# A recurrent layer's front: where the mixed inputs lie, how the second factors run, and how the 32-token blocks are inverted

## The chip, the core and the metric

The kernel runs on one core of a Trainium2 chip. The metric is the device time of one execution in microseconds (us), the median of several runs. Five engines work side by side, each through its own queue in order: TensorE (PE, its weight loads as PEld), VectorE (DVE), ScalarE (ACT), GpSimd (POOL) and SyncE (SP), which issues the loads of the weights.

## The reference, cut

Two blocks follow each other; the second one and most of the first are not touched by the change. What it touches is the time mix of the first block's first layer:

```python
xx = jnp.pad(h, ((0, 0), (1, 0), (0, 0)))[:, :-1] - h
xm = h[None] + xx[None] * mix[:, None, None, :]
xr, xw, xk, xv, xa, xg = xm[0], xm[1], xm[2], xm[3], xm[4], xm[5]
r = xr @ w_r; k = xk @ w_k; v = xv @ w_v
w_log = -jax.nn.softplus(-(w0 + jnp.tanh(xw @ w1) @ w2)) - 0.5
a = jax.nn.sigmoid(a0 + (xa @ a1) @ a2)
kk = (k * k_k).reshape(B, T, H, N)
kk = kk / jnp.maximum(jnp.sqrt(jnp.sum(kk * kk, axis=-1, keepdims=True)), 1e-12)
k = k * (1.0 + (a - 1.0) * k_a)
decay = jnp.exp(-jnp.exp(w_log))
y = wkv7_scan(r, decay, k, v, -kk, kk * a)   # a step for each token, 16 heads of 64
```

There are 272 tokens (16 meta tokens and 256), a width of 1024, 16 heads.

## The kernel before, in words

All activations lie transposed: 128 features on the partitions, 8 tiles `k` or `m` of the width, 272 tokens as columns. A large matrix product is made of *units*. A unit loads 128x1024 weights (`wf`, a ring of 5), ScalarE rounds them to a high part (`wh`, a ring of 4, L173), VectorE takes the difference as a low part (`wl`, a ring of 3, L182), and TensorE runs 24 matmuls, three for each of 8 tiles (L261 to L263). Mixed inputs are split into a high and a low part in the same way: the rounding is ScalarE's, the difference VectorE's (L488). The high part of a unit is made four units ahead, so it waits until an earlier unit has given its buffer back.

The scan over tokens is computed in chunks of 64 tokens. In each chunk the inverse of a unit triangular 64x64 matrix is wanted for every head. The kernel takes it apart into two diagonal blocks of 32 tokens and the square below them. `aab` (L737, L740, eight of them, m = 0 to 7) makes the blocks from the removal keys, `meta` the 16-token block of the meta tokens; `inverses` inverts all 32-token blocks of all heads and chunks at once on VectorE, row by row (`rows`, L862 and L865, and L879 for the last rows); and `doubles` joins two inverted blocks to 64 tokens with two products (`da`, L1116, and `db`, L1124). Behind the joining the chunks follow on TensorE, and all of it waits for it.

The *front* is what lies between the norm and the joining. Its steps stand in a list `ORDER` written out by hand, in which the chunk steps, the units of keys (`k0` to `k7`), values (`v0` to `v7`) and `r` (`r0` to `r7`) and the small steps are strung together. The queues are then ordered from that list by a scheduler, which may move instructions past others where nothing depends.

The steps that matter here:

- `low_rank`, then `lwa`, `lg1`, `lg2`: first factors of decay, rate and gate, and the hyperbolic tangents behind them (L592 to L599).
- `first_mix`: the key's mixed input. A tile is normalised (L529), the difference to the token before is written to `xx` (L531), the mixed tile is `xx * mix + hn` (L533), and it is split (L534, L488). The pair lies in a store with the tag `AR`, the same store in which the decays and unit keys are put later, so the decays' exponentials (`decay_b`, L662 and L663) come behind the last key (`dropk`).
- `mv` and `mr`: mixed inputs of values and of `r`, a tile each; the values from `xx` (L504), `r` from two scaled copies of `hn` (L501, L502).
- `l2w`, `l2a`: second factors of decay and rate (L636), two units that each load the same weights `rk_l2` and use one half of their rows.
- `evk`, `evkb`: a key's square and copy (L616, L239), its heads' squared sums (L623) and their maximum with 1e-24 (L624).
- `decay_a`: sums of the decays along the tokens (L651).
- `units`, `keys`, `keysb`, `removal`, `over`, each for a half (4 tiles) of the width: unit keys (L680, L681, L683), keys times rate (L690, L698), removal keys (L711, L713, L716) and the products with the inverse decays (L705, L707), which `aab` reads.
- `evr`, `evrb`: an `r` unit's read-out and bonus (L777, L778, L786); `solve0` to `solve8`: the steps of `inverses`.

PSUM has 8 buffers, the temporary tiles `t` 3, `s` 4.

## Time and profile before

| what | us |
|---|---|
| median of 3 runs (1541.54 to 1544.8) | 1543.73 |
| the profiled execution | 1541.39 |
| its span, first to last instruction | 1539.4 |
| PE busy, share of the span | 1477.2, 96% |
| DVE busy | 1008.7, 66% |
| ACT busy | 747.2, 49% |
| POOL busy | 263.5, 17% |
| mean granted clock | 0.984 |

All times of instructions below come from the one profiled execution; 2.0 us of its time lie around the span. A busy PE counts instructions in flight, and matmuls overlap, so a mean duration of a matmul is longer than the distance to the next one. An instruction's duration holds a start-up that overlaps with its neighbour, so the distance from one start to the next is what a queue pays. Float32 matmuls leave two records each, the ones with rounded parts (fp32r) one.

### The profile page before, as it was taken

How to read it: one execution, taken by the hardware profiler on the slowest of the kernel's cores; microseconds unless marked ns; L12 is line 12 of the kernel's file. 1: busy time of each engine (PE TensorE's matmuls, PEld its weight loads, DVE VectorE, ACT ScalarE, POOL GpSimd, SP SyncE). 2: the span in 40 equal slices, each digit the busy share in tenths (PEclk: the TensorE clock that was granted, in tenths of full speed). 3: DMA queues.
4: the chain of work that ended last, by engine and by line, in shares of the span. 5: the costliest groups of instructions: out<-in, count | busy, mean ns of one | idle time of the engine just before them, and what ended most of it. 6: DMA issues, size and time to landing. Idle time of an engine off the chain costs nothing.

```text
span 1539.4 us, 31043 instructions
## 1 busy us (share of the span) xinstructions
PE 1477.2 (96%) x12652; PEld 1404.3 (91%) x12652; DVE 1008.7 (66%) x1893; ACT 747.2 (49%) x1295; POOL 263.5 (17%) x298
## 2 busy tenths in 40 slices
PE   7999999678999999999999998999999999999999
PEld 7999998677789999999999986789999988899999
DVE  6657567996666555556555489576665589887643
ACT  6545436633255444444444344555454236666532
POOL 2111000111012111011110234141110344310000
PEclk9999999888999999999999999999999999999999
DMA  7655643222105555555555531065556543265553
GB/s 221 219 175 177 194 130 122 72 83 70 43 2 183 174 179 167 171 196 177 169 172 168 179 124 55 28 198 194 185 182 181 185 142 95 90 221 191 188 194 98
DMA packets 71874, 230.62 MB, mean 150 GB/s; under 512 B 8851, under 2 KB 13492, under 8 KB 71604
## 3 DMA queue, kind: packets, MB, share of 16 engines
q1 hardware_dynamic: 69504, 225.35, 45.4%
q10 hardware_dynamic: 2228, 3.29, 0.9%
q8 instruction: 99, 1.62, 0.4%
q14 instruction: 43, 0.35, 0.1%
HBM read 226.52 MB, written 2.10 MB: 149 GB/s over the span
## 4 chain that ended last, share of the span: by engine, by line
PE 84%; DVE 9%; ACT 3%; DMA 1%; issue 1%; POOL 1%; SPq 0%; DVEq 0%; POOLq 0%; ACTq 0%
PE mm L261 23%; PE mm L263 23%; PE mm L262 23%; PE mm L1890 1%; DVE wl L182 1%; PE mm L1164 1%; PE mm L1163 1%; PE mm L1165 1%; DMA wf<-ffn_in 1%; PE mm L1867 1%; PE mm L988 1%; PE mm L1892 1%; PE mm L1834 1%; PE mm L801 1%; ACT L L1846 1%
## 5 line engine op out<-in xcount | busy, mean ns | idle before, releaser
L173 ACT ACTIVATE wh<-wf 128x1024 fp32r<-128x1024 f32 (+2 forms) x410 | 417.7, 1020 | 549.3 <-issue 264.7
L182 DVE TENSOR_TENSOR wl<-wf,wh 128x1024 fp32r<-128x1024 f32 (+2 forms) x402 | 479.5, 1194 | 142.2 <-PE mm L263 104.0
L261 PE MATMUL mm<-xh,wh 128*128 128x272 f32 (+1 forms) x1824 | 525.7, 288 | 8.3 <-ACT wh L173 8.3
L263 PE MATMUL mm<-xh,wl 128*128 128x272 f32 (+1 forms) x1824 | 523.6, 288 | 2.7 <-DVE wl L182 2.6
L262 PE MATMUL mm<-xl,wh 128*128 128x272 f32 (+1 forms) x1824 | 523.1, 287 | 0.0
L261 PEld LDWEIGHTS mm<-xh,wh 128*128 128x128 f32 x1824 | 345.2, 189 | 11.1 <-ACT wh L173 9.2
L263 PEld LDWEIGHTS mm<-xh,wl 128*128 128x128 f32 x1824 | 344.7, 189 | 4.4 <-DVE wl L182 3.9
L262 PEld LDWEIGHTS mm<-xl,wh 128*128 128x128 f32 x1824 | 344.4, 189 | 0.4
L261 PE MATMUL mm<-hh,wh 128*128 128x272 f32 (+1 forms) x704 | 201.7, 287 | 0.0
L263 PE MATMUL mm<-hh,wl 128*128 128x272 f32 (+1 forms) x704 | 201.6, 287 | 0.0
L262 PE MATMUL mm<-hl,wh 128*128 128x272 f32 (+1 forms) x704 | 201.5, 287 | 0.0
L352 POOL TENSOR_TENSOR s<-s,rstd 128x272 f32<-128x272 f32 (+1 forms) x88 | 75.4, 859 | 443.6 <-ACT s L351 443.6
L261 PEld LDWEIGHTS mm<-hh,wh 128*128 128x128 f32 x704 | 132.6, 188 | 0.0
L263 PEld LDWEIGHTS mm<-hh,wl 128*128 128x128 f32 x704 | 132.5, 188 | 0.0
L262 PEld LDWEIGHTS mm<-hl,wh 128*128 128x128 f32 x704 | 132.4, 188 | 0.0
L360 DVE TENSOR_TENSOR u<-mm,s 128x272 f32<-128x272 f32 (+1 forms) x88 | 38.5, 437 | 118.5 <-PE mm L263 103.2
L182 POOL TENSOR_TENSOR wl<-wf,wh 128x1024 fp32r<-128x1024 f32 (+3 forms) x44 | 85.3, 1943 | 114.7 <-PE mm L263 38.6
L298 POOL TENSOR_TENSOR acc<-acc,sq 128x272 f32<-128x272 f32 (+1 forms) x48 | 41.8, 871 | 253.6 <-ACT sq L296 245.3
L350 DVE TENSOR_TENSOR t<-mm,rstd 128x272 f32<-128x272 f32 (+1 forms) x88 | 38.2, 436 | 66.9 <-PE mm L263 66.8
L261 PE MATMUL mm<-hid,wh 128*128 128x256 f32 x256 | 72.0, 281 | 0.0
L262 PE MATMUL mm<-hid,wh 128*128 128x256 f32 x256 | 72.0, 281 | 0.0
L263 PE MATMUL mm<-hid,wl 128*128 128x256 f32 x256 | 72.0, 281 | 0.0
(492 smaller groups left out, 2313.8 us busy)
## 6 DMA issues: line engine op xcount, KB each, us to landing
wf<-ffn_in SPq DMA_DIRECT2D x176, 512.0 KB, 3.6
wf<-ffn_out SPq DMA_DIRECT2D x64, 512.0 KB, 3.6
wf<-b_ff SPq DMA_DIRECT2D x64, 512.0 KB, 4.4
wf<-ffn_out SPq DMA_DIRECT2D x32, 384.0 KB, 3.2
wf<-rk_k SPq DMA_DIRECT2D x8, 512.0 KB, 3.5
wf<-rk_v SPq DMA_DIRECT2D x8, 512.0 KB, 3.3
wf<-rk_r SPq DMA_DIRECT2D x8, 512.0 KB, 3.4
wf<-rk_o SPq DMA_DIRECT2D x8, 512.0 KB, 3.3
```

Source lines behind the costliest of these rows:

```text
L173: self.A.activation(u.wh, u.wf[:u.p, :u.n], AF.Copy)
L182: (self.V if u.lo == "V" else self.G).tensor_tensor(u.wl, u.wf[:u.p, :u.n], u.wh.bitcast(F32), op=ALU.subtract)
L261: self.mm(out, wh, xh, start=start, stop=False)
L262: self.mm(out, wh, xl, start=False, stop=False)
L263: self.mm(out, wl, xh, start=False, stop=stop)
L298: self.G.tensor_tensor(self.acc[:, :n], self.acc[:, :n], self.sq[:, :n], op=ALU.add)
L350: V.tensor_tensor(t[:, :n], st.pop(("g", m))[:, :n], r, op=ALU.mult)
L352: G.tensor_tensor(s[:, :n], s[:, :n], r, op=ALU.mult)
L360: V.tensor_tensor(u[:, :n], st.pop(("u", m))[:, :n], st.pop(("s", m))[:, :n], op=ALU.mult)
L801: mm(p[:, :T], wf[:w, s], R["lo"][1 - z][:w], start=z == 0, stop=z == 1)
L988: mm(ps[h][:, j * w:(j + 1) * w], flat(src(c, m)[OWN[h]]), R["AR"][OWN[h], m, j0:j0 + n, tok(c)], start=True, stop=True)
L1163: self.mm(out, xh, wh, start=start, stop=False)
```

## The change

Four edits and a new order.

1. *Key's mixed input.* Its high part gets a slot of its own (`xkh`) and its low part the lower half of the store for the key products (now two halves, `kb0` and `kb1`). The store `AR` is free from the start, so `decay_b` stands behind the fourth key.
2. *No token differences.* Keys, values and `r` are all mixed as `mix * hn_before + (1 - mix) * hn`: a scaled copy on ScalarE and one instruction on VectorE. The tables `1 - mix` are written by GpSimd (`others`) over columns of `vec` that are no longer read.
3. *Second factors in one unit.* `l2` loads the weights once and issues a product for decay and one for rate for each tile.
4. *The maximum with 1e-24* becomes a Relu of the sum less 1e-24 on ScalarE, and 1e-24 is added again in the logarithm.
5. *Inverses in 16-token blocks.* `rows` runs 15 rows, each one instruction pair over both 16-token diagonal blocks. Then the lower square is filled: transposes (`turned`), 128 products of 32x16 (first of them the lower square times the first inverse), a copy and a transpose (`joined`), 192 products, and three instructions that add (`added`).

In the key products `aover` (removal keys) and `over` (keys) are now separate steps, and the meta columns are made for each half.

```diff
-ORDER = ("lwa k0 lg1 k1 evk0 l2w evk1 evkb0 k2 lg2 tri mv mv k3 evk2 evkb1 decay_a mv mv l2a k4 evk3 evkb2 mv k5 evk4 "
+ORDER = ("k0 lwa k1 evk0 k2 lg1 evk1 evkb0 l2 evk2 evkb1 k3 decay_a lg2 tri evk3 evkb2 decay_b k4 mv evk4 evkb3 units0 "
...
+        def mixed(i, k):
+            p, x = self.tmp("s"), self.tmp("t")
+            A.activation(p, R["hn"][:, k, :T], AF.Copy, scale=self.v("mix", 8 * i + k))
+            V.scalar_tensor_tensor(x, R["hn"][:, k, 1:], self.v("mix", 8 * MIX[i] + k), p, op0=ALU.mult, op1=ALU.add)
+            return x
...
-            x2 = R["pool"].tile([128, 2, KT, T], F32R, tag="AR", name="xk")
-            hi, lo = R["x", 2] = x2[:, 0], x2[:, 1]
+            hi = slot("xkh", F32R, (128, KT, T))
+            lo = R["half"](0, "xkl", F32R).rearrange("p (k t) -> p k t", k=KT)
...
-                eng(E("xx%d" % k)).tensor_tensor(xx[:, k], hn[:, k, :T], hn[:, k, 1:], op=ALU.subtract)
...
-                V.tensor_scalar(R["rn"][:, m], ss[:, :T], 1e-24, None, op0=ALU.max)
+                A.activation(R["rn"][:, m], ss[:, :T], AF.Relu, bias=self.eps[:, 4:5])
...
+                    ps = [self.psum() for _ in range(2)]
+                    for p, r in zip(ps, OWN):
+                        mm(p[:, :T], wf[r, m * 128:m * 128 + 128], R["lo"][0][r], start=True, stop=True)
+                    ev_w(m, ps[0][:, :T])
+                    ev_a(m, ps[1][:, :T])
...
             for s in range(s0, s1):
-                if s < B - 5:
...
+                m, w = n - 1 - s, s + 1
+                u = self.tmp("u")[:, :2 * m * w].rearrange("p (b i j) -> p b i j", b=2, j=w)
+                below = both(t, w, 0, (B, m), (1, w))
+                V.tensor_tensor(u, both(a, s, w, (1, m), (0, w)), both(t, s, 0, (0, m), (1, w)), op=ALU.mult)
+                V.tensor_tensor(below, below, u, op=ALU.add)
...
+        def turned():
+            tf, Dg, Dt = R["tf"], R["Dg"], R["af"]
+            V.transpose(Dg[:, :n], tf[:, :, :n].rearrange("p s t -> p t s"))
+            V.transpose(Dt, tf)
+            p = R["p16"] = self.psum()
+            for c in range(32):
+                for r in quads:
+                    mm(p[r, c * n:c * n + n], Dg[r, :, c], Dg[r, :n, c], start=True, stop=True)
+        def joined():
...
+            V.transpose(Dg[:, n:], tf[:, :, n:].rearrange("p s t -> p t s"))
+            self.A.activation(tf[:, :, :n], byblk(R.pop("p16")), AF.Copy)
+            G.memset(tf[:, :, n:], 0.0)
+            p, o = R["p16"] = self.psum(), self.psum()
+            for c in range(32):
+                for r in quads:
+                    mm(p[r, c * n:c * n + n], tf[r, c], Dt[r, n:, c], start=True, stop=True)
+                for r in quads[::2]:
+                    mm(o[r, c * n:c * n + n], Dt[r, :, c], tf[r, c, :n], start=True, stop=True)
...
-        cuts = (0, 5, 10, 15, 20, 25, 31)
+        cuts = (0, 5, 10, 15)
```

Three places of the queues show what moves. The first is ScalarE, behind the tangents of decay and rate. Before, the exponentials (L662, L663) stand behind the last keys, after them and a load of the function table; `wh` is a high part, `s` and `kf` a key's square and copy, `kbx` the store of squared sums:

```order
L173 ACTIVATE wh<-wf 128x1024
L616 ACTIVATE s<-mm,vec 128x272
L239 ACTIVATE kf<-mm 128x272
L301 ACT_TABLE_LOAD
L680 ACTIVATE kbx<-kbx 128x1088
L173 ACTIVATE wh<-wf 128x1024
L662 ACTIVATE AR<-pinv 128x8x272
```

In the changed kernel (its own line numbers) the same stretch of ScalarE starts behind the tangents of both factors; L639 are the Relus, L534 the scaled copies, L515 the roundings of the values' mixed input, L674 and L675 the exponentials:

```order
L534 ACTIVATE s<-hn,vec 128x272
L639 ACTIVATE kb<-mm,eps 128x272
L303 ACT_TABLE_LOAD
L674 ACTIVATE AR<-pinv 128x8x272
L175 ACTIVATE wh<-wf 128x1024
L630 ACTIVATE s<-mm,vec 128x272
L241 ACTIVATE kf<-mm 128x272
L534 ACTIVATE s<-hn,vec 128x272
L515 ACTIVATE xmh<-t 128x272
L534 ACTIVATE s<-hn,vec 128x272
L639 ACTIVATE kb<-mm,eps 128x272
L675 ACTIVATE pinv<-pinv 128x8x272
```

The exponentials have moved ahead of the fifth key's square, and the values' mixing stands between the keys' squares.

The second place is VectorE at the end of the solve. Before, the last rows (L865, L879) are mixed with read-outs of `r` units (L777, L778) and a low part, and two transposes (L885, L886) end it:

```order
L862 TENSOR_TENSOR u<-af,tf 128x81
L865 TENSOR_TENSOR tf<-tf,u 128x2x27
L777 SCALAR_TENSOR_TENSOR s<-mm,vec,kf 128x272
L778 TENSOR_TENSOR AR<-mm,AR 128x272
L865 TENSOR_TENSOR tf<-tf,u 128x3x27
L182 TENSOR_TENSOR wl<-wf,wh 128x1024
L879 SCALAR_TENSOR_TENSOR tf<-tf,af 128x28
L1048 TENSOR_TENSOR room<-mm,pc 128x256
L879 SCALAR_TENSOR_TENSOR tf<-tf,af 128x28 x3
```

In the changed kernel the last rows (L900, L901) stand beside the low parts of the last tiles of `r`'s mixed input (L504), the transposes are L909 and L910, and the first read-outs of `r` (L792, L793) come behind them:

```order
L901 TENSOR_TENSOR tf<-tf,u 128x2x3x13
L504 TENSOR_TENSOR xl<-t,xh 128x272 x2
L900 TENSOR_TENSOR u<-af,tf 128x56
L504 TENSOR_TENSOR xl<-t,xh 128x272
L901 TENSOR_TENSOR tf<-tf,u 128x2x2x14
L900 TENSOR_TENSOR u<-af,tf 128x30
L901 TENSOR_TENSOR tf<-tf,u 128x2x15
L909 STREAM_TRANSPOSE tf<-tf 128x512
L910 STREAM_TRANSPOSE af<-tf 128x1024
L792 SCALAR_TENSOR_TENSOR s<-mm,vec,kf 128x272
```

The third is TensorE at the joining. Before, the fifth `r` unit ends, a chunk product (L1042) follows, and L1116 is the next:

```order
L262 MATMUL mm<-xl,wh 128x272
L263 MATMUL mm<-xh,wl 128x272
L1042 MATMUL mm<-UV,KBt 64x64 x8
L1116 MATMUL mm<-tf,Tt 32x32 x16
L1042 MATMUL mm<-UV,KBt 64x64 x8
L1116 MATMUL mm<-tf,Tt 32x32 x8
L786 MATMUL mm<-s,mats 128x272
```

In the changed kernel the first new batch (L914) stands behind the second `r` unit, with a bonus product (L801) and the third unit behind it:

```order
L264 MATMUL mm<-xl,wh 128x272
L265 MATMUL mm<-xh,wl 128x272
L914 MATMUL mm<-tf 32x16 x128
L801 MATMUL mm<-s,mats 128x272
L263 MATMUL mm<-xh,wh 128x272
L264 MATMUL mm<-xl,wh 128x272
```

The second batch (L924 and L926 in turn, 32 times four and two) stands behind that third unit and the meta products (L1055); then come the fourth unit, two chunk products (L1067, L1084), two bonus products, the fifth unit, L1095 (which was L1042) and L1168 (which was L1116). So the whole solve lies between the second and the fifth `r` unit on TensorE, and from L1168 on both queues hold the same instructions.

## Rows read from the trace of the kernel before

**Rows 1.** Table by stage: busy us (and records) per engine, then PEclk.

```profile
core 0: us, PE busy (x) PEld busy (x) DVE busy (x) ACT busy (x) POOL busy (x), PEclk, DMA share, GB/s
220.00:230.00 10.00, 10.00 (x82) 10.00 (x82) 9.76 (x26) 1.73 (x4) 0.00 (x0) 1.00 0.00 1
229.60:291.56 61.96, 50.42 (x339) 45.89 (x337) 49.33 (x96) 46.40 (x85) 4.01 (x8) 0.93 0.35 117
...
302.45:357.35 54.90, 39.27 (x612) 36.53 (x613) 53.89 (x208) 15.67 (x28) 8.96 (x14) 0.85 0.28 87
357.35:371.31 13.96, 12.38 (x188) 10.30 (x188) 5.04 (x14) 7.37 (x13) 4.16 (x4) 0.61 0.01 2
```

**Rows 2.** What TensorE waited for, 215 to 372 us: total, times, longest.

```profile
PE mm L737 <- DVE AR L716: 12.5, 2, 9.1
PE mm L786 <- DVE s L777: 8.1, 1, 8.1
PE mm L1116 <- DVE tf L885: 5.9, 1, 5.9
```

**Rows 3.** VectorE's groups, 216 to 366 us: busy us, mean ns, idle before.

```profile
L182 DVE TENSOR_TENSOR wl<-wf,wh 128x1024 fp32r<-128x1024 f32 x21 | 25.5, 1219 | 8.7 <-issue 5.2 <-PE mm L263 2.0 <-ACT wh L173 1.4
...
L865 DVE TENSOR_TENSOR tf<-tf,u 128x110 f32<-128x110 f32 (+32 forms) x54 | 11.8, 253 | 0.1
L862 DVE TENSOR_TENSOR u<-af,tf 128x110 f32<-128x110 f32 (+32 forms) x54 | 11.5, 256 | 0.0
...
L624 DVE TENSOR_SCALAR kbx<-mm 128x272 f32<-128x272 f32 x8 | 3.5, 432 | 0.3 <-PE mm L623 0.3
...
L531 DVE TENSOR_TENSOR kbx<-hn 128x272 f32<-128x272 f32 x8 | 3.4, 440 | 0.0
...
L885 DVE STREAM_TRANSPOSE tf<-tf 128x1024 f32<-128x1024 f32 x1 | 1.9, 1905 | 0.0
...
L879 DVE SCALAR_TENSOR_TENSOR tf<-tf,af 128x28 f32<-128x28 f32 (+3 forms) x10 | 1.8, 231 | 0.0
```

**Rows 4.** VectorE's timeline before the fifth block: start, us, instruction.

```profile
295.23 1.30 DVE L698 TENSOR_TENSOR kf<-kf,kbx 128x1088 f32<-128x1088 f32 x1
296.43 1.30 DVE L711 SCALAR_TENSOR_TENSOR tha<-tha,AR 128x1088 f32<-128x1088 f32 x1
297.63 0.51 DVE L502 SCALAR_TENSOR_TENSOR t<-hn,hv,s 128x272 f32<-128x272 f32 x1
298.04 0.80 DVE L488 TENSOR_TENSOR xl<-t,xh 128x272 fp32r<-128x272 f32 x2
...
300.29 1.44 DVE L705 TENSOR_TENSOR kbx<-tha,pinv 128x256 f32<-128x256 f32 x4
...
301.96 1.43 DVE L716 TENSOR_TENSOR AR<-AR 128x252 f32<-128x252 f32 x4
```

**Rows 5.** ScalarE's timeline behind the first keys: start, us, instruction.

```profile
239.13 1.06 ACT L173 ACTIVATE wh<-wf 128x1024 fp32r<-128x1024 f32 x1 [3.62 <-PE mm L262]
240.09 0.47 ACT L616 ACTIVATE s<-mm,vec 128x272 f32<-128x272 f32 x1
...
240.74 2.00 ACT L645 ACTIVATE pinv<-mm,hv 128x272 f32<-128x272 f32 x5
```

**Rows 6.** ScalarE's groups, 216 to 366 us, columns as in rows 3.

```profile
L690 ACT ACTIVATE kbx<-tha,hv 128x272 f32<-128x272 f32 x8 | 4.3, 600 | 3.8 <-DVE AR L683 3.8
...
L501 ACT ACTIVATE s<-hn,vec 128x272 f32<-128x272 f32 x8 | 3.9, 511 | 0.0
...
L663 ACT ACTIVATE pinv<-pinv 128x2176 f32<-128x2176 f32 x1 | 2.0, 2017 | 0.0
```

**Rows 7.** Narrow float32 products in TensorE's timeline: start, us, instruction, records.

```profile
324.04 0.69 PE L1002 MATMUL mm<-AR,kbx 64*16 64x16 f32 x64
...
343.09 1.07 PE L1031 MATMUL mm<-room,Tm 16*16 16x64 f32 x32
...
370.76 0.62 PE L1124 MATMUL mm<-af,H 32*32 32x32 f32 x16
```

**Rows 8.** The weight loads of L1116, group of 216 to 366 us.

```profile
L1116 PEld LDWEIGHTS mm<-tf,Tt 32*32 32x32 f32 x80 | 2.6, 144 | 6.1 <-issue 6.0
```

**Rows 9.** Table by stage for 14 matmuls of an `r` unit at 1.2 GHz.

```profile
364.89:368.29 3.40, 3.40 (x14) 3.15 (x14) 0.00 (x0) 0.54 (x2) 0.00 (x0) 0.50 0.02 5
```

More of the change, by code (lines that the diff above doesn't have):

```diff
@@ L138, in __init__ @@
         self.later = [(mats, io["mats"]), (self.tri, io["tri"])]
-        self.eps = self.const.tile([128, 2], F32, name="eps")
+        self.eps = self.const.tile([128, 5], F32, name="eps")
         nc.vector.memset(self.eps[:, 0:1], EPS)
         nc.vector.memset(self.eps[:, 1:2], 64e-5)
+        nc.vector.memset(self.eps[:, 3:4], 1e-24)
+        nc.vector.memset(self.eps[:, 4:5], -1e-24)
     def unit(self, *a, **k):
@@ L628, in k_unit, with l2_unit @@
             self.unit(io["rk_k"][m], D, proj(2, m, "k"), lo=E("lok%d" % m), hi=E("hik%d" % m))
-        def l2_unit(j, evac, gen, after=()):
-            r = OWN[j]
+        def l2_unit():
             def fn(wf):
                 for m in range(KT):
-                    p = self.psum()
-                    mm(p[:, :T], wf[r, m * 128:m * 128 + 128], R["lo"][0][r], start=True, stop=True)
-                    evac(m, p[:, :T])
-                    if gen:
-                        next(gen)
-            self.unit(io["rk_l2"], D, fn, after, lo=None)
+                    ps = [self.psum() for _ in range(2)]
[3 more added lines that the diff above has]
+                    ev_a(m, ps[1][:, :T])
+            self.unit(io["rk_l2"], D, fn, lo=None)
         def ev_w(m, p):
@@ L658, in decay_b @@
         def decay_b():
-            AR = R["AR"] = R["pool"].tile([128, NP, 2, T], F32, tag="AR", name="AR")
-            pinv = R["pinv"][:, :, :T]
+            pinv, AR = R["pinv"][:, :, :T], R["AR"]
             with tc.issue_after(R["logs"].ins):
@@ L716, in removal_keys, with removal_over @@
                 V.tensor_tensor(a[:, :, 1:], a[:, :, 1:], p[:, :, :CH - 1], op=ALU.mult)
+        def removal_over(q):
+            over(V, 0, R["tha"], slice(4 * q, 4 * q + 4))
         def keys_over(q):
@@ L835, in rwkv @@
         for q in range(2):
-            for n, fn in (("units", units), ("keys", keys), ("keysb", keys2), ("removal", removal_keys), ("over", keys_over)):
+            for n, fn in (("units", units), ("keys", keys), ("keysb", keys2), ("removal", removal_keys), ("aover", removal_over), ("over", keys_over)):
                 steps[n + str(q)] = lambda fn=fn, q=q: fn(q)
@@ new lines, in rows @@
+                V.tensor_tensor(below, below, u, op=ALU.add)
+        quads = [slice(32 * q, 32 * q + 32) for q in range(4)]
+        byblk = lambda p: p.rearrange("p (c j) -> p c j", j=n)
+        def turned():
[6 more added lines that the diff above has]
+                    mm(p[r, c * n:c * n + n], Dg[r, :, c], Dg[r, :n, c], start=True, stop=True)
@@ new lines, in added @@
+        def added():
+            Dg, Dt = R["Dg"], R["af"]
+            p, o = R.pop("p16")
+            x = Dt[:, n:].rearrange("p t c -> p c t")
+            V.tensor_tensor(x, byblk(p), x, op=ALU.add)
+            for r in quads[::2]:
+                x = Dg[r, :n].rearrange("p t c -> p c t")
+                V.scalar_tensor_tensor(x, byblk(o)[r], self.eps[r, 2:3], x, op0=ALU.mult, op1=ALU.add)
+        def end():
+            R["D1"], R["Dt"] = R["Dg"], R["af"]
+            Tt = R["Tt"]
+            Dt = R["Dt"].rearrange("p t (m c) -> p m c t", c=NC)
@@ L912, in meta @@
                 G.tensor_copy(R["Tm"][:, :, 8 * i:8 * i + 8], x[i][:, :, :KT].rearrange("p t m -> p m t"))
-        cuts = (0, 5, 10, 15, 20, 25, 31)
-        return [start, meta] + [lambda a=a, b=b: rows(a, b) for a, b in zip(cuts[:-1], cuts[1:])] + [end]
+        cuts = (0, 5, 10, 15)
+        return [start, meta] + [lambda a=a, b=b: rows(a, b) for a, b in zip(cuts[:-1], cuts[1:])] + [turned, joined, added, end]
     def chunks(self, R):
@@ L1082, in early @@
         def early():
-            z = R["pool"].tile([128, 2, KT, T], F32R, tag="kbx", name="z")
-            R["z"] = z[:, 0], z[:, 1]
+            z = R["z"] = [R["half"](i, "z", F32R).rearrange("p (k t) -> p k t", k=KT) for i in range(2)]
             e = tok(NC - 1).start
             for q in range(2):
-                self.split(z[:, 0, qs[q], :e], z[:, 1, qs[q], :e], R["bb"][q][:, :, :e], (V, G)[q])
+                self.split(z[0][:, qs[q], :e], z[1][:, qs[q], :e], R["bb"][q][:, :, :e], (V, G)[q])
         steps = {"early": early}
```

92 lines of the change are left out of this document (43 added, 49 removed), and 10 rows, old and new, of the table ORDER.

## The prediction

> **What bounds the kernel now.** I read the table by stage first [rows 1], then what TensorE waited for [rows 2], then the groups of VectorE [rows 3]. TensorE is the bound of nearly the whole program; the exception is the front of the time mix, from 229.6 us (first matmul of a key) to 357.35 us (first product that joins 32-token blocks, L1116). In its first part TensorE is busy 50.42 of 61.96 us, in its last 39.27 of 54.90 us, while VectorE there is busy 53.89 of 54.90 [rows 1]. The waits say the same: 12.5 us in L737 for the removal keys, 8.1 us in L786 and 5.9 us in L1116 for VectorE [rows 2]. After 357.35 the order of both kernels is the same matmul for matmul, so the gain is how much earlier L1116 (L1168 in the new code) starts, plus what the same work takes behind it: 13.96 us up to the first L988 at 371.31, at a granted clock of 0.61 [rows 1], so much of it at 1.2 GHz after the wait of 5.9 us.
>
> **The change part by part.** VectorE loses the differences (L531, 3.4 us) and the maxima (L624, 3.5 us) [rows 3]. The rows of the inverse took 11.8 + 11.5 + 1.8 = 25.1 us [rows 3]: 108 instructions with 96 elements on average (5166 over 54 a side), 0.22 us each, and ten short ones. Now there are 30 with 91 on average (1360 over 15 a side): 30 x 0.21 = 6.3 us. The transposes stay even (one of 1024 in L885's 1.9 us becomes two of 512). ScalarE takes over 16 scalings (8 for the key, 8 for the value) and 8 squared sums.
> One load of 0.5 MB less on SP's queue and the factor tables on GpSimd, written ahead of the front, I cost at nothing: the longest waits there name no transfer [rows 2].
>
> *First, to the first-half removal keys.* The key's mixing ends some 2 us earlier, and three keys then run without a break: 72 matmuls at 0.122 (82 in 10.00 us, [rows 1]) from 229.6, so to 238.4. From 236.9, when the first key is through and the fifth key's high part gets its buffer, ScalarE is the longest queue. What it has up to the keys of the first half (L702): 8 high parts at 0.95 (next start 240.09 behind 239.13), 8 squares with copies at 0.65, 16 tanh at 0.375, 11 scalings at 0.41, 8 roundings at 0.32, two exponentials at 1.9, two passes over 1088 at 1.0, four keys at 0.5 [rows 5, 6], 7 relus at 0.36 taken as such a tanh, a table load 1.3 and a 0.3: 7.6 + 5.2 + 6.0 + 4.5 + 2.6 + 3.8 + 2.0 + 2.0 + 2.5 + 1.6 = 37.8 us, and 1.7 us in which the eighth key's high part waits for TensorE: 276.4 us. Queued behind ScalarE are the values' mixed inputs, so TensorE, done with the keys at 264.4, runs the first three values only as they come, to 276.6.
>
> *Second, to the fifth block product.* From 276.4 VectorE is the longest: 4 low parts at 1.13 [rows 3], three passes over 1088 at 1.2, three copies, 7 mixings, 4 unit keys, and of the key products (L705) four groups of four at 0.33 apiece with their meta pieces, less the last three, and two groups of L716 at 1.45 [rows 4]: 4.5 + 3.6 + 1.1 + 2.5 + 1.7 + 5.0 + 2.9 = 21.3 us. Block 0 may start at about 282 (before 291.6), block 4 at 297.8; before it started at 302.45. Of 9 us at the first only 4.6 are left at the second, since the other half's keys come after. TensorE waits some 5 us ahead of block 0 and 7 ahead of block 4.
>
> *Third, to the first new product.* TensorE from 297.8: block 4, the meta block and its wait 2.1, three blocks 2.9, a value at 1.2 GHz behind the wait 4.4 (14 matmuls took 3.4 at that clock, [rows 9]; at the full one 82 took 10.00, so 24 take 2.9, [rows 1]), three values 8.8, two r units 5.9, two chunk products 3.8: 27.9 us, so 325.7. VectorE meanwhile: blocks and masks to 307, a transpose 2.0, the rows 6.3, the rest of the meta block 1.8, three low parts 3.4, three mixings 2.3, small pieces 1.4, a half transpose 1.0: 325.2 us. They are level; the wait of 8.1 us goes, and nothing as long takes its place.
>
> *Fourth, TensorE alone, to the joining.* New are 128 products (L914) and 192 (L924, L926), 32 rows by 16 columns in float32, of two records each. No row is like them. The nearest from below is L1002, 16 columns: 64 records in 0.69 us, 0.022 us a product. From above L1124, 32 rows and 32 columns, one operand read across as here: 16 records in 0.62, 0.07 to 0.077 a product [rows 7]. Half of L1124's columns gives 0.035, which I take, as the operand and the height are L1124's: 4.5 and 6.7 us (bounds 7 and 24 us for both). Around them one r unit 2.9, two more 5.9, a bonus product 0.5 and two 1.0, meta products 0.7, chunk products 1.9, 1.1 and 0.7: 4.5 + 6.7 + 14.7 = 25.9, so L1168 starts at 351.6, 5.7 us earlier. Copies and memset between the two batches (some 4 us on ScalarE, VectorE and GpSimd) lie beside the r unit, the added pieces beside the next two; without that cover they would cost about those 4 us each time.
>
> *Fifth, behind the joining.* VectorE is done 8 us before L1168, so no wait of 5.9, no drop of the clock, and ScalarE has its four copies behind it. The same matmuls then take 9.8 us for 13.96: 4.1 us less.
>
> Sum: 5.7 + 4.1 = 9.8 us. Each of the eight values' tiles now goes ScalarE, VectorE, ScalarE, VectorE; for hand-offs that my sums leave out I take off 0.2 us a tile, a choice, 1.6 us. That is 8.2 us off the profiled execution's 1541.4: **1533.2**. This execution was the quickest shown; the runs' median is 2.3 higher. Forecast on the middle of both: **1534.5 us**.
>
> A rule of the Trainium skill speaks against the small blocks. L1002's 64 records at 2.4 GHz took 0.011 us apiece with 16 columns, though L1031's took 0.033 with 64 [rows 7]: there the price goes with the columns. The Trainium skill, "TensorEngine Tiling (Array Packing)", section "Instruction Overhead", says that each matmul has about 60 cycles of overhead, so that one column takes as long as 60. By that rule, as an estimate from its figure, 640 records would cost 25 ns each, 16 us and not 11.2. The trace disagrees for L1002, and would agree for L1124 against L1031, where 32 and 64 columns cost the same.
>
> **The rivals.**
> (a) *The products cost by the piece, not by the column.* In [rows 7] L1124 takes as much for 32 columns as L1031 for 64. With a price between, 0.05 a product, the 320 cost 16 us, 4.8 more: about 1539, no change that can be told. (The rule of the Trainium skill's page "TensorEngine Tiling (Array Packing)" gives this case.) Against it: L1002.
> (b) *The products pack like L1002.* Four row groups follow one another, at 0.022: 4.2 us less than the forecast: 1530. For it: the loop over quarters is innermost; against: operands read across.
> (c) *ScalarE holds the front.* Nine microseconds of work went to an engine that was busy 46.40 of 61.96 us [rows 1]. If the key mixing or the hand-offs make its chain 4 to 5 us longer, block 4 starts at 302 as before, and what is left is the shorter solve less the products: 1539. For it: every low part, relu and mixing on VectorE then waits for one queue.
> (d) *Slower: the loads of the strided weights stay in the open.* L914 and L926 load 32 columns that lie 32 elements apart; a load of L1116 lasts 0.144 [rows 8], hidden there. If for these 192 it is not hidden, they cost 0.144 apiece and the other 128 0.035: 32 us, 21 more than the forecast: 1555. Slower from about 0.08 a product on. Against it: in the rows of narrow products the loads are hidden everywhere.
> (e) *The change does not do what it says:* VectorE's four-dimensional patterns run at half the pace, the solve saves 12 and not 19 us, L914 waits for VectorE: 5 us, 1540.
>
> **How the numbers follow.** Forecast 0.52, (b) 0.14, (a) 0.11, (c) 0.11, (d) 0.08, (e) 0.04. A measurement of this kernel tells 0.2%, about 3.1 us, from no change. The forecast with its own range, 1530 to 1539, lies on the faster side but for its edge; with (b) and the lower parts of (a) and (c) that gives faster 0.72, the same 0.18 (most of (a), (c), (e)), slower 0.10 ((d), and a bad end of (c)). The range reaches down to (b) with 3 us for the sums and up to (a), (c) and (e) with 3 above: 1527 to 1543; (d) is left out.
>
> **What would show it.** Block 0 some 9 us earlier and block 4 some 4 to 5 us earlier; ScalarE without gaps from 237 to 276; no wait of 8 us on a VectorE instruction of the r units; the two batches at 4 to 5 and 6 to 7 us; the first L1168 at about 352 us of the span and no clock of 0.61 behind it. Wrong first of all if the batches take over 16 us together, or if TensorE's waits ahead of blocks 0 and 4 come to over 20 us.

## The result, and the profile after

The changed kernel is slower. Its runs took 1551.0 to 1559.2 us, median 1556.4; the kernel before took 1541.5 to 1544.9 on the same chip, median 1544.3; the ratio is 1.0071, with a 95% interval of 1.0046 to 1.0097. The forecast was 1534.5, in a range of 1527 to 1543. The execution in the trace is the quickest of the changed kernel, 1551.0 us with a span of 1549.2, against 1541.4 and 1539.4 before.

The table by stage of the changed kernel, in the columns of [rows 1] (busy us and records per engine, then PEclk, DMA share and GB/s), cut at block 0, block 4, the first batch of narrow products (L914), its end, the second batch (L924, L926), its end, the first product that joins 32-token blocks (L1168, before L1116) and the first L1041 (before L988):

```profile
core 0: us, PE busy (x) PEld busy (x) DVE busy (x) ACT busy (x) POOL busy (x), PEclk, DMA share, GB/s
230.47:284.94 54.47, 46.41 (x315) 41.76 (x313) 38.04 (x69) 48.12 (x93) 2.83 (x8) 0.97 0.30 95
284.94:300.87 15.93, 7.10 (x217) 6.80 (x217) 15.93 (x37) 4.15 (x9) 0.00 (x0) 0.76 0.35 107
300.87:330.55 29.68, 28.12 (x416) 26.47 (x416) 28.21 (x101) 14.15 (x29) 8.48 (x16) 0.90 0.24 73
330.55:335.78 5.23, 4.06 (x257) 3.93 (x257) 4.94 (x7) 1.45 (x2) 0.00 (x0) 0.86 0.20 56
335.78:342.44 6.66, 6.66 (x90) 6.25 (x91) 2.00 (x4) 1.18 (x2) 0.53 (x1) 0.60 0.40 119
342.44:352.22 9.78, 6.53 (x393) 6.37 (x385) 2.52 (x6) 0.47 (x1) 0.00 (x0) 0.78 0.20 59
352.22:367.78 15.56, 13.32 (x132) 12.02 (x132) 8.84 (x13) 6.98 (x9) 4.43 (x4) 0.81 0.13 35
367.78:378.80 11.02, 10.66 (x191) 9.19 (x187) 5.44 (x15) 3.93 (x10) 0.00 (x0) 0.85 0.17 52
```

What TensorE waited for in the changed kernel, 226 to 368 us, in the columns of [rows 2]:

```profile
PE mm L752 <- DVE kb L719: 11.4, 2, 8.8
PE mm L637 <- ACT s L630: 4.3, 4, 1.4
PE mm L926 <- issue: 2.3, 1, 2.3
PE mm L1084 <- DVE room L243: 2.1, 1, 2.1
PE mm L264 <- DVE xl L504: 1.3, 1, 1.3
PE mm L914 <- issue: 1.2, 1, 1.2
PE mm L924 <- issue: 1.0, 1, 1.0
PE mm L650 <- ACT kf L241: 0.9, 1, 0.9
```

The waits of 8.1 and 5.9 us of [rows 2] are gone, as they were meant to be. Three new ones say "issue": TensorE stood still inside the batches and waited for nothing that the profile shows. And the granted clock is 0.60 in the unit behind the first batch. VectorE's part went as forecast: the rows over 15 tokens (L900, L901) took 7.6 us (forecast 6.3) where [rows 3] had 25.1.

```profile
L900 DVE TENSOR_TENSOR u<-af,tf 128x30 f32<-128x30 f32 (+7 forms) x15 | 3.8, 256 | 0.1
L901 DVE TENSOR_TENSOR tf<-tf,u 128x30 f32<-128x30 f32 (+7 forms) x15 | 3.8, 251 | 0.1
```

The walk of the prediction against the trace, in us of the span:

| | before | forecast | after |
|---|---|---|---|
| block 0 | 291.6 | 282 | 284.9 |
| block 4 | 302.5 | 297.8 | 300.9 |
| first narrow product | – | 325.7 | 330.6 |
| joining (L1116, now L1168) | 357.35 | 351.6 | 367.8 |
| first L988, now L1041 | 371.3 | 361.5 | 378.8 |

At the first narrow product the forecast was 5 us off. The next stage, forecast at 25.9 us, took 37.2: here the gain turned into a loss.

For the rest I split TensorE's time from the first matmul of a key (229.58 before, 230.47 after) to the joining into four terms: *waits* on another engine, *stalls* ("issue"), *half clock* (for each two neighbouring matmuls of a unit that start 0.15 to 0.32 us apart, what lies over the 0.122 us of the full clock), and the *rest*, its work. The forecast's own terms: waits 3.4 (the first three values, 12.2 us for 8.8) + 5 + 7, half clock 4.4 - 2.9. Some expectations below name half clock of 3.2, 9.8 and 10.3 us; they count a few matmuls at the full clock with it, 0.5 to 1 us, which are left out here.

| us | whole | waits | stalls | half clock | rest |
|---|---|---|---|---|---|
| before | 127.8 | 30.5 | 0 | 2.3 | 95.0 |
| forecast of after | 122.0 | 15.4 | 0 | 1.5 | 105.1 |
| after | 137.3 | 20.6 | 4.4 | 8.9 | 103.4 |

So 15.3 us were missed: 7.4 of half clock, 5.2 of waits, 4.4 of stalls, less 1.7. The experiments ask what makes each. The two main theories: (1) the 320 narrow products cost more than their columns, through the number of their instructions; (2) the new front and its order lose.

### The profile page after: what moved, and what is told of

Same layout as the page of the kernel before. It is cut to its first block, busy times and chain, and to the rows that moved or that the text cites. A ratio compares the mean times of both kernels' runs of the same rounds, so it can differ in the third digit from the quotient of the medians.

```text
span 1549.2 us, 32257 instructions
## 1 busy us (share of the span) xinstructions
PE 1491.3 (96%) x13292; PEld 1418.2 (92%) x13292; DVE 996.0 (64%) x1797; ACT 757.6 (49%) x1320; POOL 260.2 (17%) x302
## 4 chain that ended last, share of the span: by engine, by line
PE 84%; DVE 9%; ACT 3%; DMA 2%; issue 2%; POOL 0%; SPq 0%; DVEq 0%; ACTq 0%; POOLq 0%
PE mm L263 23%; PE mm L265 23%; PE mm L264 23%; DVE wl L184 2%; PE mm L1942 1%; DMA wf<-ffn_in 1%; PE mm L1216 1%; PE mm L1215 1%; PE mm L1217 1%; PE mm L1919 1%; PE mm L1041 1%; PE mm L1944 1%; PE mm L1886 1%; PE mm L816 1%; ACT L L1898 1%
## 5 line engine op out<-in xcount | busy, mean ns | idle before, releaser
L263 PEld LDWEIGHTS mm<-xh,wh 128*128 128x128 f32 x1824 | 346.5, 190 | 12.8 <-ACT wh L175 10.4
L352 DVE TENSOR_TENSOR t<-mm,rstd 128x272 f32<-128x272 f32 (+1 forms) x88 | 38.2, 435 | 67.3 <-PE mm L265 67.2
```

The costliest lines, as they stand in the source:

```text
L263: self.mm(out, wh, xh, start=start, stop=False)
L352: V.tensor_tensor(t[:, :n], st.pop(("g", m))[:, :n], r, op=ALU.mult)
```

## Experiments

**Which part loses: each half of the change alone.** e1 is the changed kernel with the 32-token rows of before put back (`solve5` to `solve8` as before). e2 is the kernel before with the 16-token inverse alone, its batches at the same `r` units:

```
-solve4 solve5 evv1 solve6 solve7 evv5 solve8 v7 evv6 r0 evv7 ck0 evr0 dropv cv0 cm0 r1 evrb0 co0 r2
-evr2 evr1 cs01 cs00 evrb2 r3 r4
+solve4 evv1 evv5 v7 evv6 r0 evv7 ck0 evr0 dropv cv0 cm0 r1 solve5 evrb0 co0 r2
+evr2 solve6 evr1 r3 solve7 solve8 cs01 cs00 evrb2 r4
```

> The changed kernel with the inverse of the kernel before put back (rows over 32 tokens on VectorE, no narrow products); the new front, the key's mixing and the new order stay. Theory 1 (the loss lies in the 320 narrow products: they cost 5.2 and 9.6 us, with stalls in which TensorE waits for nothing that the profile shows, and leave the clock at half behind them): without them TensorE saves about 15 us and some 7 us of half clock, VectorE gets 19 us of rows back, so the first product that joins 32-token blocks starts at 350 to 354 us of the span (367.8 with the products) and the time is 1534 to 1540 us, ratio to the kernel before 0.994 to 0.998. Rival 1 (the loss lies in the new front and its order): blocks as in the changed kernel, but the time stays above 1548 us, ratio over 1.003. Rival 2 (VectorE was the limit there after all): the start of the joining comes at 364 us or later, since VectorE has 19 us more, and the time is 1548 to 1556.

> The kernel before with the 16-token inverse alone (rows over 15 tokens, the two batches of 128 and 192 narrow products at the same r units as in the changed kernel); front, key mixing and order ahead of it are those of before. Theory 1 (narrow products): TensorE loses its waits of 8.1 and 5.9 us on VectorE but pays 15 us for the products and some 7 us of half clock: the joining starts at 362 to 368 us (before 357.35), 4 us are won behind it, and the time is 1545 to 1552 us, ratio 1.001 to 1.005, with stalls of 1 to 2 us inside the batches as in the changed kernel. Rival 1 (the front and its order lose): the time is 1534 to 1541 us, ratio 0.994 to 0.998.

Measured: e1 1544.1 us, ratio 1.0002 (0.9985 to 1.0020); e2 1544.9 us, 0.9998 (0.9978 to 1.0017). Neither theory had these times, though e2's joining (363.7 us of the span) and its stalls came as theory 1 had them: each half alone is nothing that can be told (up to 0.2% by the intervals), both together lose 0.7%, and 0.5% in e4 and e5 below, which have as many instructions. In e1 the joining comes 127.5 us behind the first key, as before, and the waits tell why:

```profile
PE mm L752 <- DVE kb L719: 11.7, 2, 9.2
PE mm L637 <- ACT s L630: 4.3, 4, 1.4
PE mm L263 <- ACT xh L515: 3.2, 1, 3.2
PE mm L1045 <- DVE room L243: 2.7, 1, 2.7
PE mm L1129 <- DVE tf L899: 2.2, 1, 2.2
```

Of the 30.5 us of waits 26.8 are still there, in other places, and half clock takes 5.7 us for 2.3. So the new front frees next to nothing for TensorE. In e2 the joining comes at 133.5 us: the waits fall from 30.5 to 18.0, but the batches take 5.0 and 9.1 us, 3.45 of them stalls. This is also why the halves do not add up: with the old front the small blocks take 12.5 us of waits away (30.5 to 18.0), with the new one 6.2 (26.8 to 20.6), and the batches cost 14 to 15 us in both.

**What the products cost: half as many, other weights, twice the columns, woven in.**

```
 e3  for c in range(0, 32, 2): mm(p[r, c*n : c*n + 2*n], Dg[r, :, c], Dg[r, :n, c:c+2] ...)
 e4  mm(p[r, c*n : c*n + n], Dg[r, c], Dg[r, :n, c])          # and Dt[r, c] in L926
 e5  w = min(c + 2, 32); mm(p[r, c*n : w*n], Dg[r, :, c], Dg[r, :n, c:w] ...)   # all 320
 e6  self.accum(..., weave): behind each three matmuls of r3 and of r4, next(weave) four times
```

e3 leaves out the weights of every other block and e4 takes other elements, so both compute something else than the reference. e6 also moves steps of the order by a unit.

> The changed kernel with half as many narrow products, each over twice the columns (64 and 96 products of 32 columns, weights of every other block only, so half of the blocks get wrong inverses): the same columns, half the instructions. Theory 1a (what counts is the number of instructions, 82 to 137 a microsecond in the batches against 17 in a unit of weights): the batches fall from 5.2 and 9.6 us to 2.5 to 3.5 and 3.5 to 5 us, no stall over 0.5 us inside them, and the time falls by 7 to 14 us to 1540 to 1546. Theory 1b (the columns or the operands read across cost it): batches as long as in the changed kernel within 1 us, time 1550 to 1557.

> The changed kernel with the weights of the first batch and of its 64 products of the second that read across blocks (L914, L926) taken from contiguous columns instead of columns 32 elements apart (the wrong elements, so the inverses are wrong): the same instructions, no strided weight loads. Theory 1 (number of instructions): nothing moves, batches of 5.2 and 9.6 us within 0.7, time 1550 to 1557. Rival (d) of the prediction (loads of the strided weights stay in the open): the batches shorten by 3 us or more together, and the time falls to 1546 or lower.

> The changed kernel with the same 128 and 192 narrow products, but each 32 columns wide instead of 16 (the second 16 are overwritten by the next product, so the result is the same): the same instructions, twice the columns. Theory 1a (the batches are paced by the number of instructions): they take 5.2 and 9.6 us as before within 1 us, with the stalls, and the time is 1550 to 1557 us. Theory 1b (columns): 3.75 us of work in the first and 6.3 in the second double, so the batches take 9 and 15 us and the time is 1559 to 1567.

> The changed kernel with the same 320 products woven into two r units, 16 or 24 products behind each three wide matmuls of the unit, instead of in two batches: the same instructions, in a stretch that has at least 48 instructions of long matmuls among them (the order of the units behind moves by one). Theory 1a, in the form that instructions arrive at a limited pace: the stalls of 1.2, 1.0 and 2.3 us go (none over 0.5 us), the units there keep a granted clock of 0.9 or more, and the time falls by 5 to 9 us to 1543 to 1547. Rival (each such product has its price on TensorE wherever it stands): the stalls come in pieces, the sum stays within 2 us, and the time is 1550 to 1557.

Measured: e3 1543.0 us, 0.9996 (0.9975 to 1.0017); e4 1552.0, 1.0048 (1.0028 to 1.0067); e5 1552.7, 1.0053 (1.0031 to 1.0075); e6 1555.5, 1.0074 (1.0048 to 1.0101). The table by stage of e5 (first batch, what lies between, second batch), and the same three of e3:

```profile
335.54:340.59 5.05, 4.33 (x258) 4.17 (x257) 3.81 (x6) 1.48 (x2) 0.00 (x0) 1.00 0.40 110
340.59:344.82 4.23, 4.23 (x90) 3.97 (x90) 1.93 (x4) 1.18 (x2) 0.52 (x1) 1.00 0.42 125
344.82:354.40 9.58, 7.32 (x393) 6.93 (x385) 2.52 (x6) 0.47 (x1) 0.00 (x0) 0.73 0.20 60
```

```profile
334.34:336.39 2.05, 2.05 (x129) 2.00 (x129) 2.02 (x4) 1.45 (x2) 0.00 (x0) 1.00 0.00 0
336.39:340.98 4.59, 4.29 (x90) 3.96 (x91) 4.59 (x7) 1.56 (x2) 0.53 (x1) 1.00 0.52 132
340.98:346.12 5.14, 3.53 (x193) 3.36 (x193) 2.63 (x7) 0.10 (x1) 0.00 (x0) 0.76 0.56 194
```

Twice the columns in as many products (e5): 5.05 and 9.58 us, the same batches. Half the products with the same columns (e3): 2.05 and 5.14 us, with one stall of 1.6 us left in the second, where none over 0.5 was expected. So the columns are all but free, and the number of instructions is the price. Weights that lie in a row (e4) leave the batches as long as they were (5.5 and 9.4 us), but not because nothing moved. The groups of the narrow products in the changed kernel, then the same in e4 (busy us, mean ns, idle before):

```profile
L914 PE MATMUL mm<-tf 32*32 32x16 f32 x256 | 4.1, 204 | 1.4 <-issue 1.2 <-DVE tf L909 0.3
L924 PE MATMUL mm<-af,tf 32*32 32x16 f32 x256 | 6.4, 194 | 1.0 <-issue 1.0
L926 PE MATMUL mm<-tf,af 32*32 32x16 f32 x128 | 6.4, 205 | 2.3 <-issue 2.3
```

```profile
L914 PE MATMUL mm<-tf 32*32 32x16 f32 x256 | 2.8, 185 | 3.0 <-issue 2.8 <-DVE tf L909 0.3
L924 PE MATMUL mm<-af,tf 32*32 32x16 f32 x256 | 5.2, 194 | 1.6 <-issue 1.6
L926 PE MATMUL mm<-tf,af 32*32 32x16 f32 x128 | 5.2, 186 | 2.5 <-issue 2.5
```

The work fell by 2.5 us (4.1 and 6.4 to 2.8 and 5.2), so the strided loads do cost something, some 0.013 us a product and not the 0.11 that rival (d) added; and the stalls grew by as much, from 4.4 to 6.8 us. Work that is saved inside a batch comes back as a stall: something else sets its length.

The places of the stalls tell what is waited for. In the changed kernel the first comes behind 248 of the 256 matmul records of the first batch; eight are left, as the timeline shows (start, us, instruction, records, idle before):

```profile
334.01 0.29 PE L914 MATMUL mm<-tf 32*32 32x16 f32 x8
335.47 0.31 PE L914 MATMUL mm<-tf 32*32 32x16 f32 x8 [1.17 <-issue]
335.71 0.82 PE L801 MATMUL mm<-s,mats 128*128 128x272 f32 x1
```

The second comes behind 157 records of the second batch, and 8 + 90 + 157 = 255 lie between (the 90 are those of the row 335.78:342.44). The third comes 128 records later, counted in e4, where none is missing. In e5 the places are the same. In the family of e2, whose order ahead of the batches is another, they are 183 in the first batch and 251 and 379 in the second, again 128 apart. Each matmul record has its weight load, so 128 records are 256 instructions. The page of the profile counts the packets of a queue for instructions, 99 before and 104 after, and TensorE's records:

```profile
PE 1491.3 (96%) x13292; PEld 1418.2 (92%) x13292; DVE 996.0 (64%) x1797; ACT 757.6 (49%) x1320; POOL 260.2 (17%) x302
q8 instruction: 104, 1.70, 0.5%
```

2 x 13292 over 104 is 255.6: a packet of this queue is 256 instructions of TensorE, and the 1280 instructions of the 320 products are the five packets more. The same queue (packets, MB) in the 21 us ahead of the first batch, and in the 22 us of the batches:

```profile
q8 instruction: 3, 0.05, 1.0%
q8 instruction: 5, 0.08, 1.9%
```

So TensorE's code comes in packets of 256 instructions, and a run of narrow float32 products (two records, four instructions each) empties a packet in 128 x 0.015 = 1.9 us, while the packets of the second batch started 3.7 and 4.0 us apart (at 343.57, 347.31 and 351.32 us). The first change of packet inside a batch shows no stall or a short one (0.3 us in e4), the next ones do; e3's first batch, of 128 records, has none.

The trace has the time of every packet, and they show what a stall waits for. In the changed kernel three packets landed at 333.88, 344.56 and 348.73 us, and the stalls ended at 335.47, 345.93 and 350.21: 1.6, 1.4 and 1.5 us later. Over the 15 profiles that have them there are 37 such stalls in the batches, and each of the 37 ended 1.2 to 1.6 us behind the landing of a packet; the next packet started 1.0 us or more after that. So the stalls are the wait for code, and in the batches its queue did not run ahead of TensorE. The Trainium skill, "Runtime: NRT & Kernel Launch", section "Instruction fetch mechanics", has the blocks of 256 instructions and says that crossing from one to the next is mostly hidden; here it was not: the 37 stalls took 0.25 to 2.75 us.

e6 agrees in one half: woven into units, no stall is left. But the time did not fall. The first batch with its unit, the short stretch behind it, which holds most of a wait of 2.4 us, and the second batch with its unit:

```profile
334.69:343.28 8.59, 8.59 (x289) 7.49 (x291) 5.20 (x10) 1.17 (x2) 0.00 (x0) 1.00 0.60 187
343.28:346.20 2.92, 0.62 (x64) 0.51 (x64) 2.88 (x6) 1.04 (x2) 0.48 (x1) 0.73 0.15 13
352.96:367.68 14.72, 14.72 (x407) 12.67 (x406) 0.94 (x3) 1.06 (x1) 0.00 (x0) 0.50 0.01 4
```

With TensorE busy throughout, the second stretch ran wholly at 0.50, that is at 1.2 GHz: the clock fell in the wait ahead and did not come back in the mixture. But the first stretch, at 1.00, took 8.59 us too, no less than the changed kernel's batch with its stall (5.23) and the 22 wide matmuls of the stretch at 0.122 (2.7) one behind the other: the mixture itself cost what the stall did. So my expectation of 1543 to 1547 failed by both, the clock and the mixture, and its rival, a price of such products wherever they stand, had the time (1550 to 1557); e6 does not rule it out.

**Fewer products.** The 64 products of L926 give the other orientation of what L924 gives; a transpose does it too:

```
-            mm(o[r, c * n:c * n + n], Dt[r, :, c], tf[r, c, :n], start=True, stop=True)
-            V.scalar_tensor_tensor(x, byblk(o)[r], self.eps[r, 2:3], x, op0=ALU.mult, op1=ALU.add)
+            V.transpose(Dg.rearrange("p t c -> p c t"), Dt.rearrange("p t c -> p c t"))
```

e7 has it in the changed kernel, e8 and e17 (twice the same) in the kernel of e2.

> The changed kernel with the 64 products of the second batch that give the other orientation (L926), their two adds and a half transpose replaced by one transpose of 1024 columns on VectorE behind the adding: 256 narrow products are left, in two batches of 128. Theory 1a: the second batch falls from 9.6 to 5 to 6 us and takes one stall at most, the time to 1545 to 1550. If the price lay in what stands around the batches (VectorE's pieces, the order), the time stays at 1550 to 1557.

> The kernel before with the 16-token inverse alone, as in the earlier run of that, and the 64 products of the other orientation replaced by one transpose. Theory 1a: 4 to 5 us off that run's second batch of 9.1 us, so 1538 to 1542 us, ratio 0.996 to 0.999, if nothing of VectorE comes late in its place. Rival (the gain ahead of the solve is what is missing, the products are not): within 1 us of the run with all 320, ratio 0.999 to 1.001.

> The quickest kernel so far once more (before with the 16-token inverse, 256 narrow products): 1538 to 1542 us, ratio 0.995 to 0.9985 if its first result holds, 0.999 or more if that was chance; the two stalls again where 128 matmul records of a code packet end.

Measured: e7 1546.4 us, 1.0019 (0.9996 to 1.0041), second batch 4.65 us. e8 1540.1, 0.9966 (0.9947 to 0.9986); e17 1542.4, 0.9987 (0.9968 to 1.0006). e7 and e8 came in the expected times; e17 lies between its two forecasts, and its interval reaches no change. The mean of e8 and e17 is 0.998, some 3.5 us: this version, old front and small blocks with 256 products, is quicker than the changed kernel, and probably than the one before, if by little. The batches of e17 and what lies between them:

```profile
331.75:337.05 5.30, 4.08 (x257) 3.94 (x257) 3.28 (x5) 0.00 (x0) 1.64 (x3) 0.62 0.20 37
337.05:343.18 6.13, 6.13 (x59) 5.14 (x59) 1.81 (x3) 0.60 (x1) 0.00 (x0) 0.77 0.16 61
343.18:348.39 5.21, 2.77 (x258) 2.55 (x257) 2.73 (x5) 1.06 (x1) 0.00 (x0) 0.83 0.19 69
```

Even there three stalls are left (1.2, 0.25 and 2.2 us). e7 against e8 is the same inverse behind the new and behind the old front: the new one is 0.5% slower (0.3% against e17).

**Where the new front loses.** All on the kernel of e7, but e12, on that of e8; in short (e10 also drops the 1e-24 in the logarithm):

```
 e9   -aab4 meta v4 mr aab5 evv4 aab6 aab7 mr solve0       +aab4 meta aab5 aab6 aab7 v4 mr evv4 mr solve0
 e10  -A.activation(rn, ss, AF.Relu, bias=-1e-24)          +V.tensor_scalar(rn, ss, 1e-24, None, op0=ALU.max)
 e11, e12  -"lov": "VVVVVVVV"    +"lov": "GGGGVVVV"
 e13  e10 and e11 together
 e16  e10 and -"lor": "VVVVVVVV" +"lor": "GGGVVVVV"
```

> The kernel of the run with 256 narrow products (changed kernel, other orientation by a transpose) with one piece of the order moved: the fifth value's unit stands behind block products 4 to 7 and no longer between 4 and 5. Theory 2 (half clock is paid where wide units stand right behind a wait; block products, 32 columns wide, hardly feel it): the unit behind the wait of 8.9 us ahead of block 4 lost 1.2 to 1.9 us; that loss falls below 0.7, the first narrow product comes 1 to 2 us earlier counted from the key's first matmul (100.2), and the time falls by about as much, to 1543.5 to 1546. Rival: the low clock moves along with the unit or the blocks take so much longer: no change, 1545 to 1548.

> The kernel with 256 narrow products, with the eight maxima of the keys' squared sums put back on VectorE (ScalarE's relus go). Theory 3 (in the new front ScalarE is the limit up to block 0, busy 48.1 of 54.5 us, and VectorE from there to the last block): TensorE's waits on ScalarE, 5.2 us, fall by 1.5 to 4 us, block 0 comes within 1 us of 54.1 us behind the key's first matmul, but blocks 4 and later come 0 to 3 us later, since VectorE has 3.5 us more; time within 2 us of 1546. Rival (ScalarE is the limit of the whole front): block 4 comes 2 to 4 us earlier, and the time falls to 1542 to 1544.

> The kernel with 256 narrow products, with the low parts of the first four values' weights on GpSimd, which is busy 2.8 of the first 54.5 us, and not on VectorE: 4 x 1.2 us less there. Theory 3 (VectorE's queue sets when blocks 4 to 7 may start): the wait of 8.9 us ahead of block 4 shrinks by 3 to 4.8 us, the first narrow product comes 2 to 4 us earlier, time 1541 to 1544. Rival (TensorE has nothing else to do by then, or VectorE runs slower beside GpSimd): waits in sum within 1 us, time 1545 to 1548.

> The same move of four low parts to GpSimd in the kernel before with the 16-token inverse and 256 narrow products (1540.1 us, ratio 0.9966 in its run), where VectorE is the limit from the first key to the last block. Theory 3: the waits of 9.2 and 3.0 us ahead of the block products shrink by 3 to 4.8 us together, time 1536 to 1538, ratio 0.9935 to 0.996. Rival (as in the run above): no change, ratio 0.996 to 0.998.

> The kernel with 256 narrow products with both reliefs of the two runs before at once: the maxima back on VectorE (ScalarE relieved, in the run alone block 0 came 4.8 us earlier and the first narrow product 0.6 later) and the low parts of the first four values on GpSimd (VectorE relieved, alone 1.2 us later at the first narrow product). Theory 4 (at the first narrow product TensorE's own queue, VectorE's and ScalarE's are level, so that relief of one only moves the wait): with both, the first narrow product comes 2 to 4 us earlier, at 96 to 98.5 us behind the key's first matmul, and the time is 1542 to 1545. Rival (TensorE's own work and half clock set it, 84 us of work to there): it comes at 100 to 102 us again, time 1546 to 1550.

> The kernel with 256 narrow products, the maxima on VectorE (as in the run that brought block 4 2.7 us earlier, after which VectorE's transpose came 2.6 us late for the first narrow product) and the low parts of the first three r weights on GpSimd, so that VectorE has 3.6 us less between the last block and the first narrow product. Theory 5 (the front's gain is there at block 4 and is lost to VectorE's queue behind the blocks): the waits of 2.6 us for the transpose and 2.3 us in the first r unit shrink by 3 us or more, the first narrow product comes at 97 to 98.5 us behind the key's first matmul, time 1542 to 1545.5. Rival (half clock on units of weights, 10.3 us in that run, takes what the waits give): 100 to 101.5 us again, time 1546 to 1549.

| | time, ratio (interval) | block 0 | block 4 | first narrow product |
|---|---|---|---|---|
| e7 | 1546.4, 1.0019 | 54.1 | 70.1 | 100.2 |
| e9 | 1549.7, 1.0041 (1.0022 to 1.0061) | 54.5 | 70.5 | 101.9 |
| e10 | 1549.0, 1.0025 (1.0008 to 1.0043) | 49.3 | 67.3 | 100.8 |
| e11 | 1547.2, 1.0023 (1.0005 to 1.0041) | 55.0 | 70.9 | 101.4 |
| e13 | 1547.2, 1.0016 (0.9997 to 1.0035) | 52.0 | 70.5 | 101.8 |
| e16 | 1553.0, 1.0053 (1.0032 to 1.0074) | 49.3 | 67.4 | 104.4 |
| e8 | 1540.1, 0.9966 | 60.4 | 71.3 | 98.3 |
| e12 | 1542.3, 0.9979 (0.9963 to 0.9995) | 60.5 | 71.4 | 98.4 |

(Places in us behind the first key.) My theories here fell one after another. e9, with the wide unit moved away from the wait, has as much half clock as e7 (6.3 us for 6.2), its first narrow product comes 1.7 us later and the time is longer than either forecast. e10 shows that ScalarE sets block 0 and block 4 in the new front: with eight relus off it block 0 comes 4.8 us earlier, block 4 2.7. This is rival (c) in its cause; and yet at the first narrow product nothing is left of it:

```profile
PE mm L752 <- DVE kb L719: 6.3, 1, 6.3
PE mm L637 <- ACT s L630: 3.7, 3, 1.9
PE mm L914 <- DVE tf L909: 2.6, 1, 2.6
PE mm L265 <- DVE wl L184: 2.5, 1, 2.5
PE mm L263 <- ACT xh L515: 1.3, 1, 1.3
```

Here VectorE is late for L914, and half clock takes 9.3 us for 6.2. Low parts moved to GpSimd (e11, e12) leave TensorE's waits up to block 4 as they were in sum (18.3 us for 18.1, 14.6 for 14.5), so the time that VectorE spends on these low parts is not the limit there. e13 went as its rival said, with 10.4 us of half clock. e16 made a new wait, which neither of its forecasts had: 6.4 us in an `r` unit for the high part of its mixed input, beside low parts on GpSimd. It stays open which single queue holds the new front behind block 4; shown is that an earlier block 0 is not an earlier first narrow product.

**The chance of one execution.** Both kernels once more, for a second profile.

> The kernel before once more, for a second profile of it. Theory 2a (the half clock on units of weights between the key's first matmul and the first product that joins 32-token blocks, 3.2 us in the profile of before and 9.8 in that of the changed kernel, belongs to the kernels): 2 to 4.5 us again, the joining 126.5 to 129 us behind the key's first matmul. Rival (it is the chance of an execution): 5 us or more.

> The changed kernel once more, for a second profile. Theory 2a: 8 to 11 us of half clock on units up to the joining, 136 to 139 us behind the key's first matmul, stalls of 3.5 to 5.5 us in the two batches. Rival (chance of an execution): 7 us or less, and the joining at 135 us or earlier.

Measured: before 1542.1 us, the joining 126.6 us behind the first key, half clock 2.2 us, waits 30.3. After 1549.2 us, 136.4 us, half clock 6.6 (7.4 as the expectation counts, between its two forecasts), waits 21.3, stalls 3.9. So the half clock belongs to the kernels, 2.2 and 2.3 us against 6.6 and 8.9, with 2.2 us of chance in the changed one (e4 had 8.0, e5 6.7). Either half of the change brings some: 5.7 us in e1, which has the new front and no narrow product, 5.9 in e2, which has the products and the old front. The stalls come again in the same places. The unit behind the first batch had 0.65 and, in e5, 1.00: how much is lost there differs from execution to execution.

## Why the prediction was wrong, step by step

- **What bounds the kernel:** right for before. The waits of 8.1 and 5.9 us on VectorE were real; e2, which takes only those away, has 18.0 us of waits for 30.5.
- **First and second step (blocks 0 and 4):** 284.9 for 282 and 300.9 for 297.8, with ScalarE at 48.12 of 54.47 us up to block 0 and VectorE at 15.93 of 15.93 from there to block 4, as the walk had it. What I did not weigh is its price: TensorE, which had done 50.42 us of work in the first part of [rows 1], did 46.41 up to block 0, and stood 8.8 us ahead of block 4 (before 3.3, of the 12.5 in [rows 2]). Block 0 came 6.6 us earlier, not 9, and block 4 1.6, not 4 to 5; and e1 shows that the front alone brings nothing.
- **Third step:** 29.7 us for 27.9. TensorE and VectorE were level there, as forecast (a wait of 0.3 us at L914).
- **Fourth step: the one that failed.** 25.9 forecast, 37.2 measured: 11.3 of the 16.2 us by which the joining came late. The batches took 5.2 and 9.8 us for 4.5 and 6.7, the rest 22.2 for 14.7. In the batches the price of 0.035 us a product was right for the work (3.8 and 6.3 us without stalls, 0.030 and 0.033 a product), if by luck: it came from halving L1124's price for its columns, and columns cost next to nothing (e5). The wait for code, 4.4 us, had been put at nothing. The price was taken from groups of 16 to 64 records [rows 7], shorter than a packet of code, and a price per product from a short group does not hold for a run of 256 or 384 records. I asked of the loads of weights whether they are hidden, and not of the code. In the rest, 3.6 us are half clock in its three units, 2.1 a wait for VectorE (L1084), and 1.8 were not split further. e3's step, with half the products, takes 26.1 us, close to the forecast by chance: its batches take 7.2 us and the rest 18.9.
- **The clock.** I charged half clock once up to the joining, 1.5 us, and 6.6 to 8.9 came; for the fifth step I wrote "no drop of the clock". [rows 9] and [rows 1] had shown 1.2 GHz behind waits; the new waits and the narrow batches ahead of units of wide matmuls should have had this price. By the first profile this is the largest of the terms, 7.4 of 15.3 us; by the second it is 5.1 of 14.4, and the waits are 5.9.
- **Fifth step:** 11.0 us for 9.8, at a clock of 0.85, so 2.9 us won of 4.1. Behind it 2.3 us more were lost up to the end, which I did not follow.
- **The rivals.** (a) had the right rule, a price by the piece: 16 and 32 columns cost the same (e5). Its price, 0.05, is met only with the stalls, 0.041 and 0.051 us a product. The rule of the Trainium skill that it names, "TensorEngine Tiling (Array Packing)", section "Instruction Overhead", some 60 cycles a matmul, so that one column takes as long as 60, agrees with e5 in that. As a price, 25 ns a record (an estimate from the 60 cycles at 2.4 GHz), it agrees with the second batch as a whole (9.8 us over 384) and not with e3's first (2.05 over 128, 16 ns). (b)'s 0.022 is the work where the weights lie in a row (2.8 us over 128 in e4's first batch), and the stalls hid it. (d) had the time, 1555, by luck: the strided loads cost about a tenth of what it gave them. (c) is right in its cause up to block 4 (e10), but taking it away wins nothing. (e) did not happen: the four-dimensional rows took 0.25 us each, as long as the rows before. That a batch of narrow products outruns its own code, and that the clock pays for it, stood in no rival. Of the two signs of being wrong neither came: the batches took 15.0 us together, not over 16, and the waits ahead of blocks 0 and 4 16.9, not over 20.

## What to carry to other kernels

Before wide work of an engine is traded for many small instructions of another, count the instructions as well as their columns, and take a price only from a group as long as the new one: beyond a packet of code the run is paced by its arrival. Charge the granted clock where wide matmuls follow a wait or a narrow batch. And where one step is brought forward, follow what its engine, its feeder and TensorE do instead: two halves of a change that are each worth nothing can lose together.
